# Fifteen of sixteen final scalings moved from VectorE to GpSimd, and the split of one row moved from 768/256 to 704/320

## The chip, the cores and the metric

The kernel runs on one core of one Trainium2 chip. The metric is the device time of one execution in microseconds. It is given as the median of several executions. The span in a profile is about 1.55 us shorter than the time of the same execution.

## The reference

A float32 array of 32 x 512 x 1024 is summed over its last axis and divided by 1024:

```python
def setup_inputs():
    batch, seq, dim = 32, 512, 1024
    return {"x": np.random.randn(batch, seq, dim).astype(np.float32), "divisor": float(dim)}

def reference(x, divisor):
    return (np.sum(x, axis=-1) / divisor).astype(np.float32)
```

Each of 128 partitions sums 128 rows of 1024 elements. The input is 67.11 MB and the output 64 KB.

## The kernel before

The first 112 rows of each partition go through three rotating buffers of 14 rows (`t`). The last 16 rows arrive in shrinking pieces, so that little is left to do when the last byte lands. VectorE (DVE in the profile) and ScalarE (ACT) share the sums. The last row is cut into three column pieces, pa, pb and pc.

```python
    L = 16
    bulk = ctx.enter_context(tc.tile_pool(name="bulk", bufs=3))
    one = ctx.enter_context(tc.tile_pool(name="one", bufs=1))
    # ... psum pool ...
    res = one.tile([P, M], F32, name="res")
    fin = one.tile([P, L], F32, name="fin")
    q = one.tile([P, L], F32, name="q")
    r = one.tile([P, L], F32, name="r")
    nc.gpsimd.memset(r, 0.0)
    # ... 112 rows through `bulk`; then 8 rows (in a bulk buffer), and from `one`: 4, 2 rows ...

    c = 768
    row = one.tile([P, D], F32, name="row")
    load(row, x_last[:, j, :])
    act_sum(r[:, j : j + 1], row[:, c:], by=scale)
    nc.vector.reduce_sum(out=q[:, j : j + 1], in_=row[:, :c], axis=AX)

    a, b = 448, 704
    pa = one.tile([P, a], F32, name="pa")
    pb = one.tile([P, b - a], F32, name="pb")
    pc = one.tile([P, D - b + 2], F32, name="pc")
    # ... loads of pa, pb, pc; scaling and store of the first 112 columns ...
    act_sum(pc[:, D - b : D - b + 1], pa)
    nc.vector.reduce_sum(out=pc[:, D - b + 1 :], in_=pb, axis=AX)
    nc.vector.scalar_tensor_tensor(
        out=fin[:, : L - 1], in0=q[:, : L - 1], scalar=scale, in1=r[:, : L - 1], op0=MULT, op1=ADD
    )
    scaled = one.tile([P, D - b + 2], F32, name="scaled")
    nc.vector.tensor_scalar(
        out=scaled, in0=pc, scalar1=scale, scalar2=0.0, op0=MULT, op1=ADD, accum_out=fin[:, L - 1 :]
    )
    tc.keep_in_program_order(nc.sync.dma_start(out=o_last, in_=fin))
```

The closing code, not shown, puts the last store behind a wait for GpSimd and for every load.

## Time and profile before

| | before |
|---|---|
| time | 161.4 us, median of 3 (161.34 to 161.51) |
| span of the profile | 159.8 us |
| read from HBM | 67.11 MB at 420 GB/s over the span |
| landing of the row before the last | 156.157 us |
| landings of pa, pb, pc | 156.698, 157.019, 157.501 us |
| last DVE signal | 158.295 us |
| store issued / landed | 158.312 / 159.729 us |

A landing is the last of the sixteen increments that a transfer makes to its semaphore. The trace records each increment. The page and the chain of waits are shown in the prediction. One more view is the DMA issues. Its last column is the time from the issue to the landing in microseconds, here for the last four loads of the kernel before:

```profile
row<-in_x_dram SPq DMA_DIRECT2D x1, 512.0 KB, 33.2
pa<-in_x_dram SPq DMA_DIRECT2D x1, 224.0 KB, 33.3
pc<-in_x_dram SPq DMA_DIRECT2D x1, 160.0 KB, 33.1
pb<-in_x_dram SPq DMA_DIRECT2D x1, 128.0 KB, 33.1
```

They take 33 us because some 13.6 MB of other loads (12, 8, 4 and 2 rows) are ahead of them in the queue, which is 32 us at 420 GB/s.

### The profile page before, as it was taken

How to read it: one execution, taken by the hardware profiler on the slowest of the kernel's cores; microseconds unless marked ns; L12 is line 12 of the kernel's file. 1: busy time of each engine (PE TensorE's matmuls, PEld its weight loads, DVE VectorE, ACT ScalarE, POOL GpSimd, SP SyncE). 2: the span in 40 equal slices, each digit the busy share in tenths (PEclk: the TensorE clock that was granted, in tenths of full speed). 3: DMA queues.
4: the chain of work that ended last, by engine and by line, in shares of the span. 5: the costliest groups of instructions: out<-in, count | busy, mean ns of one | idle time of the engine just before them, and what ended most of it. 6: DMA issues, size and time to landing. Idle time of an engine off the chain costs nothing.

```text
span 159.8 us, 139 instructions
## 1 busy us (share of the span) xinstructions
DVE 121.1 (76%) x17; ACT 19.6 (12%) x37; POOL 0.8 (0%) x6
## 2 busy tenths in 40 slices
DVE  0500059995999599978999599959995996494985
ACT  3000000000000000000000000000001900480973
POOL 0000000000000000000000000000000000001000
DMA  7999999978999999978999999978999999899993
GB/s 250 472 459 459 459 459 459 459 330 359 459 459 459 459 459 459 459 316 373 459 459 459 459 459 459 416 345 388 459 459 427 394 480 505 353 435 390 408 400 132
DMA packets 2592, 67.18 MB, mean 420 GB/s; under 512 B 544, under 2 KB 928, under 8 KB 1056
## 3 DMA queue, kind: packets, MB, share of 16 engines
q1 hardware_dynamic: 2592, 67.18, 98.0%
HBM read 67.11 MB, written 0.07 MB: 420 GB/s over the span
## 4 chain that ended last, share of the span: by engine, by line
DMA 76%; DVE 22%; SPq 1%; issue 0%; DVEq 0%
DMA t<-in_x_dram 56%; DMA row<-in_x_dram 21%; DVE res L153 20%; SPq L142 1%; DVE q L176 1%; DVE scaled L198 0%; DVE pc L193 0%; DVE fin L194 0%; DVEq L198 0%; DVEq L232 0%
## 5 line engine op out<-in xcount | busy, mean ns | idle before, releaser
L153 DVE TENSOR_REDUCE res<-t 128x14 f32<-128x14336 f32 (+3 forms) x9 | 111.2, 12360 | 34.3 <-DMA t<-in_x_dram 34.3
L147 ACT ACTIVATE junk<-t 128x1024 f32<-128x1024 f32 x16 | 16.2, 1013 | 135.9 <-DMA t<-in_x_dram 135.9
L153 DVE TENSOR_REDUCE q<-t 128x4 f32<-128x4096 f32 (+2 forms) x3 | 7.9, 2642 | 2.7 <-DMA t<-in_x_dram 2.5
L147 ACT ACTIVATION_READ_ACCUMULATOR junk<-t 128x1 f32 x16 | 3.0, 187 | 0.0
L147 ACT ACT_TABLE_LOAD x1 | 1.3, 1283 | 1.7 <-PEq L218 1.7
L189 POOL TENSOR_SCALAR res<-res 128x112 f32<-128x112 f32 x1 | 0.5, 494 | 143.8 <-DVE res L153 143.8
L176 DVE TENSOR_REDUCE q<-row 128x1 f32<-128x768 f32 x1 | 1.0, 953 | 0.0
L198 DVE TENSOR_SCALAR_CACHE_REDUCE scaled<-pc 128x322 f32<-128x322 f32 x1 | 0.5, 490 | 0.1
L147 ACT ACTIVATE junk<-pa 128x448 f32<-128x448 f32 x1 | 0.5, 548 | 0.0
L193 DVE TENSOR_REDUCE pc<-pb 128x1 f32<-128x256 f32 x1 | 0.4, 414 | 0.0
L147 ACT ACTIVATE junk<-row 128x256 f32<-128x256 f32 x1 | 0.4, 388 | 0.1
L194 DVE SCALAR_TENSOR_TENSOR fin<-q,r 128x15 f32<-128x15 f32 x1 | 0.2, 176 | 0.0
L147 ACT ACTIVATION_READ_ACCUMULATOR junk<-pa 128x1 f32 x1 | 0.2, 186 | 0.0
L147 ACT ACTIVATION_READ_ACCUMULATOR junk<-row 128x1 f32 x1 | 0.2, 185 | 0.0
L139 POOL MEMSET r<- 128x16 f32 x1 | 0.1, 112 | 1.3 <-POOLq L218 1.3
L218 POOL MEMSET const-bfloat16-1.0<- 128x1 bf16 x1 | 0.1, 103 | 0.0
L218 POOL MEMSET const-uint8-127<- 128x1 uint8 x1 | 0.1, 102 | 0.0
L218 POOL MEMSET const-float32-0.0<- 128x1 f32 x1 | 0.1, 99 | 0.2 <-issue 0.2
L218 POOL MEMSET const-float32-1.0<- 128x1 f32 x1 | 0.1, 99 | 0.0
L198 DVE DVE_READ_ACCUMULATOR scaled<-pc 128x1 f32 x1 | 0.1, 83 | 0.0
## 6 DMA issues: line engine op xcount, KB each, us to landing
t<-in_x_dram SPq DMA_DIRECT2D x7, 7168.0 KB, 35.7
t<-in_x_dram SPq DMA_DIRECT2D x1, 6144.0 KB, 33.3
t<-in_x_dram SPq DMA_DIRECT2D x1, 4096.0 KB, 26.1
t<-in_x_dram SPq DMA_DIRECT2D x2, 1024.0 KB, 18.6
t<-in_x_dram SPq DMA_DIRECT2D x1, 2048.0 KB, 30.5
row<-in_x_dram SPq DMA_DIRECT2D x1, 512.0 KB, 33.2
pa<-in_x_dram SPq DMA_DIRECT2D x1, 224.0 KB, 33.3
pc<-in_x_dram SPq DMA_DIRECT2D x1, 160.0 KB, 33.1
```

Of the source, the lines that this page charges most:

```text
L139: nc.gpsimd.memset(r, 0.0)
L142: tc.keep_in_program_order(nc.sync.dma_start(out=dst, in_=src))
L147: nc.scalar.activation(junk[:, :n], src, COPY, scale=by, accum_out=dst)
L153: nc.vector.reduce_sum(out=dst[:, :d], in_=t[:, :d, :], axis=AX)
L176: nc.vector.reduce_sum(out=q[:, j : j + 1], in_=row[:, :c], axis=AX)
L189: nc.gpsimd.tensor_scalar_mul(out=res, in0=res, scalar1=scale)
L193: nc.vector.reduce_sum(out=pc[:, D - b + 1 :], in_=pb, axis=AX)
L194: nc.vector.scalar_tensor_tensor(out=fin[:, : L - 1], in0=q[:, : L - 1], scalar=scale, in1=r[:, : L - 1], op0=MULT, op1=ADD)
L198: nc.vector.tensor_scalar(out=scaled, in0=pc, scalar1=scale, scalar2=0.0, op0=MULT, op1=ADD, accum_out=fin[:, L - 1 :])
L218: nc = _bacc.Bacc("TRN2", target_bir_lowering=False, num_devices=1)
```

## The change

Its intent is to take the scaling of fifteen columns out of the DVE's last two microseconds, and to shorten the DVE's part of the row before the last. The pieces of the last row stay at 448, 256 and 320 columns.

```diff
-    r = one.tile([P, L], F32, name="r")
-    nc.gpsimd.memset(r, 0.0)
+    r = one.tile([P, 1], F32, name="r")
@@
-    c = 768
+    c = 704
     row = one.tile([P, D], F32, name="row")
     load(row, x_last[:, j, :])
-    act_sum(r[:, j : j + 1], row[:, c:], by=scale)
+    act_sum(r, row[:, c:], by=scale)
@@
-    nc.vector.scalar_tensor_tensor(
-        out=fin[:, : L - 1], in0=q[:, : L - 1], scalar=scale, in1=r[:, : L - 1], op0=MULT, op1=ADD
+    nc.gpsimd.tensor_scalar_mul(out=fin[:, :j], in0=q[:, :j], scalar1=scale)
+    nc.gpsimd.tensor_scalar(
+        out=fin[:, j : j + 1], in0=q[:, j : j + 1], scalar1=scale, scalar2=r, op0=MULT, op1=ADD
     )
```

## The prediction

> **What bounds the kernel now.** I read the page first, then the chain of work that ended last in order of time, then the timeline of the last microseconds, the semaphore records of the same stretch, and the waits of the store queue. The page says what the whole span is spent on:
>
> ```profile
> span 159.8 us, 139 instructions
> DVE 121.1 (76%) x17; ACT 19.6 (12%) x37; POOL 0.8 (0%) x6
> HBM read 67.11 MB, written 0.07 MB: 420 GB/s over the span
> DMA 76%; DVE 22%; SPq 1%; issue 0%; DVEq 0%
> ```
>
> The input is streamed once at 420 GB/s, and the part of the DVE in the chain is mostly its release of the three big buffers, with the queue still full. The change touches no transfer: the last row is cut at 448 and 704 before and after, although its short description names those pieces. So up to the landing of the row before the last, at 156.16 us, nothing that counts can move. What can move is the end of the chain:
>
> ```profile
> 122.91 33.25 DMA row<-in_x_dram
> 156.16 0.02 issue
> 156.18 0.96 DVE q L176
> 157.14 0.03 issue
> 157.17 0.18 DVE fin L194
> 157.34 0.34 DVE pc L193
> 157.68 0.04 DVEq L198
> 157.72 0.07 issue
> 157.79 0.49 DVE scaled L198
> ```
>
> After the landing there are 2.1 us of DVE work in series, then the store. The timeline has the same stretch with ACT beside it (start, duration, engine, line, operation):
>
> ```profile
> 156.18 0.39 ACT L147 ACTIVATE junk<-row 128x256 f32<-128x256 f32 x1
> 156.18 0.95 DVE L176 TENSOR_REDUCE q<-row 128x1 f32<-128x768 f32 x1
> 156.50 0.18 ACT L147 ACTIVATION_READ_ACCUMULATOR junk<-row 128x1 f32 x1
> 156.72 0.55 ACT L147 ACTIVATE junk<-pa 128x448 f32<-128x448 f32 x1
> 157.17 0.18 DVE L194 SCALAR_TENSOR_TENSOR fin<-q,r 128x15 f32<-128x15 f32 x1
> 157.20 0.19 ACT L147 ACTIVATION_READ_ACCUMULATOR junk<-pa 128x1 f32 x1
> 157.26 0.41 DVE L193 TENSOR_REDUCE pc<-pb 128x1 f32<-128x256 f32 x1
> 157.79 0.49 DVE L198 TENSOR_SCALAR_CACHE_REDUCE scaled<-pc 128x322 f32<-128x322 f32 x1
> 158.31 0.34 SPq L201 DMA_DIRECT2D out_dram<-fin  x1
> ```
>
> The reader should see that the scaling of fifteen columns (L194), although written after the reduction of pb (L193), was scheduled ahead of it and stands between the two reductions. The semaphore records of the trace give the moments in between. Last increments of the loads: row 156.157, pa 156.698, pb 157.019, pc 157.501. DVE signals: L176 at 157.143, L193 at 157.683, L198 at 158.295. ACT signals: the row part at 156.697, pa at 157.398. So L193 started 0.24 us after its data, and L198 0.29 us after its last transfer: at this end the DVE is late, not the DMA. The pa part of ACT started 0.02 us after its landing: it follows the DMA.
>
> [...] The trace of before can't test this: the one GpSimd scaling runs at 145.65 with the DVE idle. [...] The trace has 494 ns for a TENSOR_SCALAR of 112 columns, which I take as the ceiling for 14 and 1 columns. [...] The trace agrees that neighbours overlap: L193 starts at 157.258, 0.086 us before L194's end at 157.344, while L194, which needs L176's result, starts 0.025 us after the signal.
>
> **The change part by part.**
>
> *Column split of the row before the last, 768 to 704 for the DVE.* The reductions of 1024, 768 and 256 elements take 1220, 953 and 414 ns, so an element costs (1220 - 953)/256 = 1.04 ns. 64 elements fewer are 67 ns: 886 ns, ending at 157.066, signal at about 157.076 in place of 157.143. On ACT the pieces of 448 and 256 take 548 and 388 ns, 0.83 ns an element; 64 more are 53 ns. The row part on ACT then signals at about 156.750, and its accumulator read ends near 156.74. In this trace ACT's next ACTIVATE can start some 0.09 us ahead of such an end (148.62 + 0.19 against 148.71), so ACT is free at 156.65, still before pa at 156.698. The pa sum stays where it is, with its signal at 157.398. This shift to ACT is free.
>
> *Scaling leaves the DVE.* L194 took 176 ns, of which 0.09 us held the next instruction; with the wait for L176's signal its removal lets L193 follow L176 directly. L193 needs nothing from L176. By the overlap above it could start at 157.066 - 0.086 = 156.98, but pb lands at 157.019. So it starts at about 157.04 and signals 0.425 us later (414 ns, as before): 157.467. Before: 157.683. The gain here is **0.216 us**, and the transfer of pb, not the DVE, now sets it. Of the split's 0.067 us, at most 0.03 us is used, since the rest ends in waiting for pb.
>
> *L198.* It waits for L193 and for ACT's pa sum (157.398, earlier), then starts 0.105 us after L193's signal (157.683 to 157.788): 157.572. Its transfer pc landed at 157.501, and with the 0.02 us seen elsewhere could release it at 157.52. So it keeps the whole 0.216 us, with 0.05 us to spare before the DMA takes over here too. Ends and signals at 158.079.
>
> *GpSimd gains two small instructions.* The first (14 columns) can go at about 156.23, 0.075 us after the DVE's signal at 156.154 (L189 started 0.074 us after its own). The second (column 14, with r as the added scalar) needs L176 at 157.076 and r at 156.750: it starts near 157.15. My estimate for each is 0.2 to 0.4 us, with 0.494 as ceiling; so they are done by 157.4 to 157.65. They stand beside L193 and are not in its path. The tile system tracks columns, not whole tiles (the DVE's sums into q didn't wait for ACT's sums into other columns of q), so L198, which writes the last column of fin, should not wait for GpSimd.
>
> *The store.* Before it the closing code makes the store queue wait for GpSimd and the earlier transfers. In the trace the last of these, the landing of the large output, comes at 157.707, and the queue stands ready at 157.776. The store's own wait for the DVE falls from 158.295 to 158.079, still later. Issue to landing took 1.417 us (158.312 to 159.729) and is left alone.
>
> *The memset of r* at 1.7 us goes; it is beside a load and worth nothing.
>
> Sum: 0.216 us off a span of 159.8, or 161.4 - 0.2 = **161.2 us**, 0.13%.
>
> **Rivals.** *A: GpSimd becomes the last to finish.* The store also needs its last result. To cost anything it must signal after 158.08 less the queue's step of some 0.05 us, so its one-column instruction would have to last 0.85 us or more from 157.15[...]. For: GpSimd's small-operand time is nowhere in the trace. Against: 112 columns took 0.494[...]. It would make it 161.3 to 161.6. *B: L198 does wait for GpSimd*, because fin has two writers now. Then it would start 0.05 to 0.1 us after 157.4 to 157.65, so at 157.5 to 157.75, and the gain would shrink to between 0.04 and 0.2 us: 161.2 to 161.36. Against: the tracking by columns shown for q. *C: the transfers hide it.* If pb and pc land some 0.1 us later after the row than in this one trace, the DVE merely waits longer and the gain falls to 0.1 us: 161.3. For: the planned starts are already within 0.02 to 0.07 us of these landings, and their spread is not known from one trace. *D: it is lost in the noise.* Three runs before spread over 0.17 us, as much as the whole effect.
>
> **Range and chances.** The centre is the full gain, since ACT and the DMA leave just enough room for it. C and B would move the time up by 0.1 to 0.15 us, the spread of a median of few runs by 0.08 us either way; a larger gain than 0.25 us is barred by pc's landing (157.501 plus the fixed rest). So 161.05 to 161.45. Two per cent is 3.2 us, more than the 2.1 us of work after the last row's predecessor has landed, so faster is all but excluded; slower would need GpSimd to hang about for 3 us. Faster 0.01, same 0.98, slower 0.01.
>
> **What would show the steps right or wrong.** In the changed profile: L176 near 886 ns, the row part on ACT near 441 ns; the reduction of pb starting within 0.05 us of pb's landing (it was 0.24 us); no two-input operation on the DVE; the last DVE instruction starting about 1.41 us after the row's landing, against 1.63 before; two GpSimd scalings under 0.5 us each, done before the last DVE instruction is; the store waiting for the DVE and not for GpSimd. I am wrong if the chain of waits goes through GpSimd, if L198 starts behind GpSimd's signal, or if the last DVE instruction still starts 1.6 us after the row's landing.

Passages that no trace of this case shows are cut from the prediction, and the cuts are marked. Three are in the paragraph behind the semaphore records: on whether DVE and GpSimd work slow each other (the remark on what the trace of before can't test is about this), on the speed of GpSimd in general, and on what the shown time of a DVE instruction contains. Two are in rival A. The sum came to 0.216 us off the span, or 161.4 - 0.2 = 161.2 us, from times of the runs and the trace of before alone. The 0.2 to 0.4 us for each small GpSimd instruction was my estimate, made with the 494 ns that the trace has for 112 columns as a ceiling. That GpSimd would not slow the DVE beside it was not shown: in that trace GpSimd scales from 145.65 to 146.14 us, and the DVE is idle from 145.57 to 147.66.

## More of the kernel before

All executions told of here were with a granted clock of 1.000.

The tiles of the pool `one` are laid behind one another in SBUF in the order in which they are declared.

## The result, and the profile after

The changed kernel took 161.44 us (median of 6, 161.36 to 161.60). The kernel before took 161.31 us in the same rounds (median of 6, 161.25 to 161.51). The ratio is 1.0008, with a 95% interval of 0.9995 to 1.0021. By its medians the changed kernel is 0.13 us slower, which this interval does not tell from no change. A ratio here is the mean time of one kernel's fast runs over that of the other's in the same rounds, so it is not quite the ratio of the medians.

By the 2% measure this is the same. Yet the forecast was 0.2 us down from the kernel before, a ratio of 0.9988, and that lies below the interval. So the expected gain is missing. Two views of the profile of the changed kernel show that nothing went wrong at the engines. First lines from its timeline (start, duration, engine, line, operation, and in brackets the idle time before with its releaser):

```profile
156.39 0.89 DVE L175 TENSOR_REDUCE q<-row 128x1 f32<-128x704 f32 x1
156.41 0.26 POOL L193 TENSOR_SCALAR fin<-q 128x14 f32<-128x14 f32 x1 [10.22 <-DVE q L152]
157.01 0.55 ACT L146 ACTIVATE junk<-pa 128x448 f32<-128x448 f32 x1
157.38 0.42 DVE L192 TENSOR_REDUCE pc<-pb 128x1 f32<-128x256 f32 x1
157.38 0.27 POOL L194 TENSOR_SCALAR fin<-q,r 128x1 f32<-128x1 f32 x1 [0.71 <-DVE q L175]
157.92 0.49 DVE L198 TENSOR_SCALAR_CACHE_REDUCE scaled<-pc 128x322 f32<-128x322 f32 x1
158.44 0.34 SPq L201 DMA_DIRECT2D out_dram<-fin  x1
```

The two-input scaling is gone from the DVE. Both GpSimd instructions end before the DVE's last one starts. The chain of the changed kernel, in order of time (start, duration, what):

```profile
123.94 33.41 DMA pb<-in_x_dram
157.35 0.02 issue
157.38 0.43 DVE pc L192
157.81 0.04 DVEq L198
157.84 0.08 issue
157.92 0.49 DVE scaled L198
```

The chain now goes straight from pb's transfer into the reduction of pb, as planned. But that transfer lands at 157.35, while it landed at 157.02 before. The DMA issues of the changed kernel say the same of all four last loads:

```profile
row<-in_x_dram SPq DMA_DIRECT2D x1, 512.0 KB, 33.4
pa<-in_x_dram SPq DMA_DIRECT2D x1, 224.0 KB, 33.5
pc<-in_x_dram SPq DMA_DIRECT2D x1, 160.0 KB, 33.3
pb<-in_x_dram SPq DMA_DIRECT2D x1, 128.0 KB, 33.4
```

Each took 0.2 to 0.3 us longer from issue to landing. The records of semaphores and instructions of the two traces close the account (microseconds):

| | before | after | difference |
|---|---|---|---|
| first landing | 4.803 | 4.836 | +0.033 |
| landing of the four-row tile | 152.471 | 152.579 | +0.108 |
| landing of the two-row tile | 154.900 | 155.079 | +0.179 |
| landing of the row before the last | 156.157 | 156.369 | +0.212 |
| landing of pb | 157.019 | 157.351 | **+0.332** |
| from pb's landing to the store's issue | 1.293 | 1.090 | **-0.203** |
| store's issue | 158.312 | 158.441 | +0.129 |

The two bold numbers sum to +0.129. The engines gave the forecast 0.2 us, and the transfers took more than that away. The delay grows step by step from the four-row tile on. The eight-row load just before it landed at 147.633 and 147.666 us, only the 0.033 us apart that the first landings already were.

The transfers have the same sizes, the same order and the same sources. What differs is where they land. The tile r shrank from 64 bytes a partition to 4. The allocator rounds that to 32 bytes, as the addresses in the built programs show. Everything declared after r that is loaded (the four-row and two-row tiles, row, pa, pb and pc) therefore moved 32 bytes down. Before, all six began on a multiple of 256 bytes. Afterwards they begin 224 bytes past one. The trace's packet records fit: the mean packet of 8192 bytes (the two-row tile's) takes 309.0 ns before and 314.3 after, and that of 1280 bytes (pc's) 55.0 and 60.9. Those of 16384 (611.3 and 615.8), 1792 (74.0 and 75.3) and 1024 bytes (46.0 and 46.6) are longer too. The row's packets, of 4096 bytes, tell nothing: single long ones sway their mean (172.1 and 161.9, with a longest of 380 and 172).

### The profile page after: what moved, and what is told of

The parts are those of the page before. It is cut to its first block, busy times and chain, and to the rows that moved or that the text cites. A ratio compares the mean times of both kernels' runs of the same rounds, so it can differ in the third digit from the quotient of the medians.

```text
span 159.9 us, 140 instructions
## 1 busy us (share of the span) xinstructions
DVE 121.0 (76%) x16; ACT 19.7 (12%) x37; POOL 1.2 (1%) x7
## 4 chain that ended last, share of the span: by engine, by line
DMA 77%; DVE 21%; SPq 1%; issue 0%; DVEq 0%
DMA t<-in_x_dram 56%; DMA pb<-in_x_dram 21%; DVE res L152 20%; SPq L141 1%; DVE scaled L198 0%; DVE pc L192 0%; DVEq L198 0%; DVEq L232 0%
## 5 line engine op out<-in xcount | busy, mean ns | idle before, releaser
L175 DVE TENSOR_REDUCE q<-row 128x1 f32<-128x704 f32 x1 | 0.9, 886 | 0.1
L198 DVE TENSOR_SCALAR_CACHE_REDUCE scaled<-pc 128x322 f32<-128x322 f32 x1 | 0.5, 489 | 0.1
L198 DVE DVE_READ_ACCUMULATOR scaled<-pc 128x1 f32 x1 | 0.1, 81 | 0.0
## 6 DMA issues: line engine op xcount, KB each, us to landing
t<-in_x_dram SPq DMA_DIRECT2D x1, 6144.0 KB, 33.3
pc<-in_x_dram SPq DMA_DIRECT2D x1, 160.0 KB, 33.3
```

Of the source, the lines that this page charges most:

```text
L198: nc.vector.tensor_scalar(out=scaled, in0=pc, scalar1=scale, scalar2=0.0, op0=MULT, op1=ADD, accum_out=fin[:, L - 1 :])
```

## The experiments

**Theory A**: the new addresses slow the transfers. **Theory B**: the transfers scatter from run to run, and this profile was a late one. **Theory C**: the GpSimd work slows the DVE beside it. All twelve runs gave correct results, and all are "same" by the 2% measure, so the argument rests on the intervals, on ranges of runs that do not overlap, and on the traces. e1 to e4 ran on one chip, e5 to e8 on a second and e9 to e12 on a third, each set with its own runs of the kernel before. Where the expectations speak of seven tiles they count the result tile `scaled` too, which no load fills; the "single one" in that of e8 does not exist; and in that of e9 the loss of 0.2 us belongs to 224 bytes and that of 0.25 to 32. In each of those of e3, e4 and e9 a passage that no run shows is cut. With it went the first case of e3: a loss that grows with the distance past the boundary, which I had put under 0.06 us at 32 bytes.

### e1: the changed kernel at the old addresses

```diff
-    r = one.tile([P, 1], F32, name="r")
+    r = one.tile([P, L], F32, name="r")[:, :1]
```

The built program has the same instructions as the changed kernel, but for the row step of r.

> The changed kernel with r 16 columns wide again (only its first is used), so that the seven tiles behind r lie where they lay before the change; the instructions are the same. Theory A (addresses): the change moved these tiles 32 bytes down, off a 256-byte boundary, their transfers became slower and landed 0.2 to 0.3 us later, which ate the 0.2 us gained on the DVE. Then this run has packets as before (55 ns for 1280 bytes, 309 for 8192), pb lands near 157.02 to 157.05, and the time is 0.2 us below the kernel before (about 161.1). Theory B (scatter of the transfers from run to run): packets and time as in the changed kernel, about 0.1 us above before, or anything between. Theory C (GpSimd beside the DVE slows it): time as in the changed kernel, with the pb reduction at 421 ns and not 414.

Measured: 161.15 us (161.03 to 161.23, 5 runs) against 161.31 of the kernel before, ratio 0.9989 (0.9977 to 1.0002). The packets are back at 309.0 and 55.0 ns. Its DMA issues:

```profile
row<-in_x_dram SPq DMA_DIRECT2D x1, 512.0 KB, 33.2
pa<-in_x_dram SPq DMA_DIRECT2D x1, 224.0 KB, 33.3
pc<-in_x_dram SPq DMA_DIRECT2D x1, 160.0 KB, 33.0
pb<-in_x_dram SPq DMA_DIRECT2D x1, 128.0 KB, 33.1
```

The old times from issue to landing are back. The time is 0.16 us below the kernel before, near the 0.2 of theory A. A miss in the expectation: pb landed at 157.147, not 157.02 to 157.05, because this profile was late by 0.13 us from its first landing on (4.931). From first landing to pc's landing it took 152.616 us, against 152.922 in the changed kernel. The pb reduction still took 420 ns, so its 7 ns more than before are not what cost the time, and theory C falls.

### e2, e3, e9, e10: the kernel before, with only the addresses moved

```diff
-    r = one.tile([P, L], F32, name="r")
+    r = one.tile([P, L + 56], F32, name="r")[:, :L]   # 224 bytes; with 8, 16 and 32 columns: 32, 64 and 128
```

> The kernel before with r widened by 56 columns, so that the same seven tiles lie 224 bytes past a 256-byte boundary, as in the changed kernel. Theory A: packets of 1280 bytes near 60 ns in place of 55, landings of the last pieces 0.2 to 0.3 us later, time 0.2 to 0.35 us above the kernel before (ratio 1.0012 to 1.002). Theories B and C: no difference from before (ratio 1.000).

> The kernel before with r widened by 8 columns: the same tiles 32 bytes past a 256-byte boundary in place of 224. [...] If any start off 64 bytes costs the same, it is as large as there: 0.2 to 0.35 us.

> The kernel before with r widened by 16 columns: the seven tiles 64 bytes past a 256-byte boundary. The two runs with 32 and 224 bytes lost 0.2 and 0.25 us, equally[...]. If what counts is being off a multiple of 64 bytes, this run is as the kernel before: 161.3, packets of 8192 bytes at 309 ns. If every start off 256 bytes costs the same: 161.5, packets at 313 to 314 ns.

> The same with 128 bytes. A multiple of 64 should cost nothing (161.3, 309 ns for 8192 bytes) if 64 is what counts; 161.5 and 313 ns if it is 256; 161.5 at 64 and 161.3 here if it is 128.

| bytes past a multiple of 256 | run | time, us (range of 5) | ratio to before (95%) | first landing to pc's, us | packet of 8192 / 1280 bytes, mean ns |
|---|---|---|---|---|---|
| 0 | kernel before | 161.31 and 161.32 | 1 | 152.698 | 309.0 / 55.0 |
| 32 | e3 | 161.56 (161.46 to 161.59) | 1.0015 (1.0002 to 1.0027) | 152.929 | 314.2 / 58.4 |
| 64 | e9 | 161.47 (161.41 to 161.50) | 1.0009 (0.9996 to 1.0021) | 152.867 | 313.0 / 58.7 |
| 128 | e10 | 161.54 (161.42 to 161.68) | 1.0013 (1.0000 to 1.0026) | 152.825 | 312.6 / 60.4 |
| 224 | e2 | 161.51 (161.48 to 161.56) | 1.0013 (1.0000 to 1.0025) | 152.948 | 314.1 / 56.7 |

The DMA issues of e2, against the 33.2, 33.3, 33.1 and 33.1 of the kernel before:

```profile
row<-in_x_dram SPq DMA_DIRECT2D x1, 512.0 KB, 33.4
pa<-in_x_dram SPq DMA_DIRECT2D x1, 224.0 KB, 33.6
pc<-in_x_dram SPq DMA_DIRECT2D x1, 160.0 KB, 33.3
pb<-in_x_dram SPq DMA_DIRECT2D x1, 128.0 KB, 33.4
```

An instruction stream that is untouched, but for the row step of r, loses 0.15 to 0.25 us by its addresses alone. The ten runs of e2 and e3 (161.46 to 161.59) all lie above the nine of the kernel before beside them (161.24 to 161.39), and the five of e1 all below. Theory A is shown, and theory B falls as the cause: each of the four moved layouts has slower packets and a longer way to pc's landing than any profile with these tiles on a boundary. The interval of e9 includes 1, those of e2 and e10 begin at it, and that of e3 is clear of it. A miss: e2's packets of 1280 bytes took 56.7 ns, where near 60 was expected.

The loss does not grow with the distance past the boundary: against the 161.31 and 161.32 of the kernel before it is 0.25 us at 32 bytes, 0.15 at 64, 0.22 at 128 and 0.20 at 224. These loads' sources start at multiples of 256 bytes of the input in every version; it is the SBUF side that moved. Of the two cases that I named for e3, the one with a loss that grows with the distance (under 0.06 us) failed and the other (0.2 to 0.35) came true with 0.25. The case in e3, e9 and e10 that a multiple of 64 bytes is enough failed as well, since 64 and 128 cost 0.15 and 0.22 us. Why such a start costs time, no run shows.

### e8: only the last three pieces back on a boundary

```diff
+    gap = one.tile([P, 8], F32, name="gap")
     pa = one.tile([P, a], F32, name="pa")
```

> The changed kernel with a gap of 32 bytes ahead of pa: pa, pb and pc on 256-byte boundaries, the four-row and two-row tiles, the single one and the row still 224 past one. From the packets' times in the two profiles (8 packets an engine for each transfer), the first group lost about 36 + 43 + 23 ns and the last three about 10 + 5 + 47, so aligning the last three should give back some 0.06 to 0.1 us of the 0.29 us that the run with r 16 wide gave back: time about 161.35. If it is the last, short transfers that matter, nearly all comes back: 161.15 to 161.2.

Measured: 161.30 us (161.21 to 161.34), ratio 0.9996 (0.9984 to 1.0008); first landing to pc's 152.795 us. Of the 0.306 us between the changed kernel (152.922) and e1 (152.616), the last three pieces give back 0.127. The other 0.179 lies with the tiles ahead of them. The forecast from packet times was low on the trace (0.06 to 0.1 us), and its time of 161.35 was near. Packet times are low for the whole as well: eight packets an engine for each transfer (128 in the trace, over sixteen engines), without the row's, make the changed kernel lose 0.14 us against e1 (16384 bytes 615.8 ns against 611.2, 8192 314.3 against 309.0, 1792 75.3 against 74.0, 1024 46.6 against 46.0, 1280 60.9 against 55.0). That is about half of the 0.306, and where the rest arises is not shown.

### e5 and e6: the two parts of the change, each alone, at the old addresses

e5 is e1 with `c = 768`; e6 is the kernel before with `c = 704`.

> One part alone, on the addresses of the kernel before: the scaling on GpSimd, the row ahead of the last still split 768 to 256. If the whole gain at the end is the scaling's leaving the DVE (my step: the reduction of pb then waits for pb's landing, and the DVE's 67 ns of the split are not needed), the reduction of pb starts within 0.05 us of pb's landing, the last DVE signal comes about 1.95 us after the row's landing (2.14 in the kernel before, 1.94 in the run with r 16 wide), and the time is that of the run with r 16 wide, about 161.15. If the split is needed too, it lies half-way: 2.0 us, 161.22.

> The other part alone: the kernel before with 704 to 320 in place of 768 to 256, the scaling still on the DVE; addresses as before. My step: the reduction of the row is 67 ns shorter and everything behind it on the DVE moves up by that, so the last DVE signal comes 2.07 us after the row's landing in place of 2.14, and the time falls by 0.07 us, to 161.24, which is inside the scatter. If ACT or a landing sets the end, nothing moves: 2.14 us and 161.31.

| | before | e6, split alone | e5, scaling alone | e1, both |
|---|---|---|---|---|
| row's landing to last DVE signal, us | 2.138 | 2.070 | 1.988 | 1.941 |
| pb's landing to store's issue, us | 1.293 | 1.218 | 1.084 | 1.084 |
| pb's landing to start of its reduction, us | 0.239 | 0.167 | 0.023 | 0.024 |
| time, us | 161.3 in each set | 161.34 (161.18 to 161.87) | 161.11 (161.01 to 161.34) | 161.15 (161.03 to 161.23) |
| ratio (95%) | 1 | 1.0005 (0.9991 to 1.0019) | 0.9989 (0.9977 to 1.0001) | 0.9989 (0.9977 to 1.0002) |

The timeline of e6 shows what stays in the way:

```profile
156.28 0.89 DVE L176 TENSOR_REDUCE q<-row 128x1 f32<-128x704 f32 x1
157.20 0.17 DVE L194 SCALAR_TENSOR_TENSOR fin<-q,r 128x15 f32<-128x15 f32 x1
157.29 0.41 DVE L193 TENSOR_REDUCE pc<-pb 128x1 f32<-128x256 f32 x1
```

The split alone takes its 67 ns off the DVE's stretch (2.070 against 2.138, as expected), but in time that is lost in the scatter: e6 is inconclusive there. The scaling alone frees the pb reduction entirely, and counted from pb's landing it is as good as both parts. Counted from the row's landing e5 looks half-way, because in that profile pb landed 0.921 us after the row, not 0.873 as in e1. e12 below, with the same 768 and a distance of 0.872, has 1.944 us (its expectation said 1.98, after e5), so these runs show no share of the split in the gain.

### e4, e7, e11, e12: the three big buffers

In both kernels the big buffers start 128 bytes past a multiple of 256. A gap ahead of them, and a wider r so that the small tiles keep to a boundary, moves them:

```diff
+    pad = ctx.enter_context(tc.tile_pool(name="pad", bufs=1))
+    gap = pad.tile([P, 32], F32, name="gap")           # e7: 24 columns
     bulk = ctx.enter_context(tc.tile_pool(name="bulk", bufs=3))
@@
-    r = one.tile([P, 1], F32, name="r")
+    r = one.tile([P, L + 32], F32, name="r")[:, :1]    # e7: 56 columns
```

e4 and e7 are the changed kernel with this, e11 is the kernel before, and e12 is e4 with `c = 768`.

> The changed kernel with every loaded tile on a 256-byte boundary: the seven small ones by a wider r, and the three big buffers by a gap of 128 bytes ahead of them (they lie 128 bytes past a boundary in both kernels). Theory A with no more to it than the last tiles: as the run with r 16 wide, 0.2 us below before. If the big buffers pay for their 128 bytes as well ([...]some 5 ns, in each of 80 packets an engine), up to 0.35 us more is gained: 0.5 us below before. Theory B: no difference from the changed kernel.

> As the run with every loaded tile on a 256-byte boundary, but the three big buffers 224 bytes past one (they lie 128 past in both kernels of the case). The last tiles are on boundaries. If the loss is one of each packet, whatever its size, the 80 large packets an engine lose 3 to 5 ns each against the fully aligned run: 0.25 to 0.4 us, time 161.25 to 161.4. If a large transfer hides it, time as the fully aligned run: 161.0.

> The kernel before with every loaded tile on a 256-byte boundary, so only the three big buffers move (128 bytes past a boundary in the kernel before). In the changed kernel the same step went with 0.15 us (161.15 to 161.00), but the time from the first landing to pc's differed by only 0.015 us in the two profiles, and 0.1 us lay before the first landing. If the big buffers' start counts: 161.15 and 152.55 us from the first landing to pc's. If that 0.15 us was scatter: 161.3 and about 152.65.

> The candidate for the best version: scaling on GpSimd, the row still split 768 to 256, every loaded tile on a 256-byte boundary. The parts so far: the scaling alone 161.11, the fully aligned one 161.00 with 704. If the big buffers' start counts: 161.0. If not, 161.1 to 161.15. Either is below both kernels of the case (161.3 and 161.4). The last DVE signal should come 1.98 us after the row's landing, as in the run with the scaling alone.

| | big buffers past a multiple of 256 | time, us (range of 5) | ratio to before (95%) | first landing to pc's, us |
|---|---|---|---|---|
| e1 | 128 | 161.15 (161.03 to 161.23) | 0.9989 (0.9977 to 1.0002) | 152.616 |
| e7 | 224 | 161.20 (161.18 to 161.26) | 0.9991 (0.9979 to 1.0003) | 152.693 |
| e4 | 0 | 161.00 (160.93 to 161.10) | 0.9980 (0.9967 to 0.9994) | 152.601 |
| e12 | 0 | 160.97 (160.94 to 161.09) | 0.9980 (0.9967 to 0.9994) | 152.547 |
| e11 (instructions of before) | 0 | 161.25 (161.12 to 161.46) | 0.9997 (0.9984 to 1.0009) | 152.551 |

What the big buffers' start is worth in time is not settled. The three profiles with it on a boundary have the shortest way to pc's landing: 152.566 us on average, against 152.639 for the four others whose small tiles are on a boundary and whose big ones are at 128 (the kernel before, e1, e5, e6). That would be 0.07 us. e11 met the first case of its expectation in the trace (152.551) and lies between both in time (161.25): it shows no more than those 0.07 us there, with a wide scatter, and e4 shows 0.15 us against e1, of which 0.1 us lies before the first landing in the profiles. e7's expectation of 161.25 to 161.4 was too high, and of the 0.5 us that e4's held possible 0.31 came.

A steadier measure shows more. Take for each landing the mean of its sixteen increments in place of the last one, and go from the first landing to that of the eight-row load, the last into a big buffer. This takes 142.82 to 142.84 us in all ten profiles with these buffers at 128, 142.62 to 142.64 in the three on a boundary, and 142.91 in e7 at 224. So the start of the big buffers counts too, by some 0.2 us there. By pc's landing 0.05 to 0.15 us of it is left (e4 against e1, e12 against e5, e11 against the kernel before). Why the rest is lost in the small transfers behind it, no run tells.

e12 and e4 are the fastest versions here; the 0.03 us between them is less than the scatter. e12 is 0.35 us below the kernel before of its rounds (160.97 and 161.32), e4 0.31, and the intervals of both stay below 1. The timeline of e12:

```profile
156.04 0.95 DVE L177 TENSOR_REDUCE q<-row 128x1 f32<-128x768 f32 x1
156.91 0.42 DVE L194 TENSOR_REDUCE pc<-pb 128x1 f32<-128x256 f32 x1
157.45 0.49 DVE L200 TENSOR_SCALAR_CACHE_REDUCE scaled<-pc 128x322 f32<-128x322 f32 x1
```

The reduction of pb follows that of the row without a gap, even with 768 columns in the latter.

## Why the prediction was right or wrong

The measured 161.44 us lies in the stated range, at its upper edge, and the chances named the right class. But the centre was 0.2 us down and the kernel went 0.13 us up, for a cause that neither the sum nor the rivals name. So that the time lies in the range is luck: the range was made for scatter and for other losses. The working must be read step by step.

**Right: the DVE part.** The row's reduction took 886 ns, as worked out, and ACT's part 441. The pb reduction started 0.024 us after pb's landing. From pb's landing to the store's issue 0.203 us were saved, where the sum said 0.216. Of the 0.013 us between them, 7 ns are the pb reduction itself (421 ns where I had 414) and 6 the step from its signal to L198 (0.111 us where I had 0.105).

**Right: GpSimd stays out of the way.** The two instructions took 262 and 267 ns, inside the estimate of 0.2 to 0.4 us. L198 did not wait for them, and neither did the store: GpSimd's signal came at 157.659 and the store's release by the DVE at 158.424. In the built program L198 waits for ACT, for the DVE and for pc's load, and not for GpSimd. Rivals A and B did not happen. As an estimate from the 495 ns of 112 columns and the 262 of 14 alone, a column costs GpSimd (495 - 262)/98 = 2.4 ns, more than twice the DVE reduction's 1.04, on top of some 230 ns fixed. The one-column instruction, with r as a second input, took 267, and spans on this engine are rough in a profile, so this is a hint.

Whether GpSimd slows the DVE a little is left open. The pb reduction took 421 ns in the changed kernel and 0.42 us in e1, e4, e5 and e12, with GpSimd work beside it, and 414 ns in the kernel before and 0.41 us in e2, e3 and e6, without. The row's 704 columns took 0.89 us with (the changed kernel) and without (e6). With the scaling on GpSimd the pb reduction also starts on an idle or just freed DVE rather than behind the two-input scaling, so no run tells the two causes apart. That GpSimd's instruction, of about 260 ns, blocks the DVE for its whole length is excluded.

**Right: the split is of little use.** e5 and e12 against e1 and e4 (161.11 and 160.97 us against 161.15 and 161.00) show no gain from it once the scaling is gone.

**Wrong: "The change touches no transfer" and "So up to the landing of the row before the last, at 156.16 us, nothing that counts can move."** This step failed, and with it the sum. The change left the loads' sizes, order and sources alone but moved the destination of six of them by shrinking a tile declared ahead of them. The row landed 0.212 us later and pb 0.332, so another 0.120 us came between the two. That spoiled the prediction's own test too: the last DVE instruction started 1.549 us after the row's landing (1.631 before), not 1.41. e1 undoes only that and comes to 161.15, where the prediction had 161.2, and there that start is at 1.433; e2 does only that to the old kernel and loses 0.20 us.

**Rival C had the right place and the wrong cause.** It said that later landings of pb and pc would eat the gain, and put it down to a scatter relative to the row. The pieces were indeed later after the row, pb by 0.120 us and pc by 0.045, but by a cause that every run of the changed kernel has. (A slip in the range: a gain over 0.25 us was called barred by pc's landing. The working's own 0.216 and 0.05 us to spare put that bar at 0.27.) The remark that the memset is "worth nothing" was about the instruction; the tile behind it was what counted.

## What to carry to other kernels

When a diff changes the size or the order of a small tile, compare the start addresses of all loaded tiles in the two built programs before forecasting anything: in this kernel, whose packets fill 98.0% of the sixteen DMA engines' span, moving six loaded tiles off multiples of 256 bytes cost 0.15 to 0.25 us in all (e2, e3, e9, e10), with packets of 8192 bytes at 312.6 to 314.2 ns in place of 309.0. Here it was enough to keep the loaded tiles on multiples of 256 bytes, by rounding the small tile ahead of them up; declaring the small tiles after them is another way, which no run tried. To judge a change of a tenth of a per cent, read the trace from a landing to the end, where the scatter of the transfers drops out, and then ask whether the landing itself moved.
